# A padded memory layout: three of the activation's four sums moved from byte 320 to byte 0 modulo 512 of their partition

## The chip, the cores and the metric

The kernel runs on one core of one Trainium2 chip. The metric is device time in microseconds (us) for one execution, from numbers already in the chip's memory to the result written back. Lower is better. Inside the core, TensorE (PE) multiplies matrices, VectorE (DVE) and ScalarE (ACT) do elementwise work, GpSimd (POOL) does a little of it and issues some transfers, and SyncE (SP) issues most transfers. On-chip memory has 128 partitions; every tile has a start byte that is the same in each partition.

## The reference

The reference is two layers of an encoder on 512 tokens of width 1024, in float32. Each layer runs

```
h = h + 0.5 * post(SwiGLU(pre(h)))      first half-step feed-forward, d_ff = 2816
u = pre(h); three attention branches and three sigmoid gates from one projection of u
h = h + post((sum_i gate_i * (branch_i @ W_branch_i)) @ W_out)
h = h + 0.5 * post(SwiGLU(pre(h)))      second half-step feed-forward

swiglu(x) = (silu(x @ Wg) * (x @ Wu)) @ Wdown
```

where `pre` and `post` are RMS norms with a gain. Everything below is about the four feed-forward parts (two layers, two in each), and there about `x @ Wg` and `x @ Wu`.

## The kernel before

**Number format.** Every float32 operand `v` is divided into a high part `hi` (v rounded to the matmul's format by a copy on ACT) and a low part `lo = v - hi` (on DVE). One block product is three matmuls: hi·hi, hi·lo, lo·hi. A matmul has a stationary operand, 128x128, loaded by LDWEIGHTS, and a moving operand that streams 256 or 512 columns past it. Loading the next stationary operand overlaps the running matmul.

**Phases.** The program runs the phases f, m, f, f, m, f: `ffn` (kind "f") and `mixer` (kind "m", the attention). Each opens a pool of tiles for itself (`open_phase`, L130) which is laid over the pool of the phase before it; a new tile waits until the old tiles at its bytes are no longer used. Pools `sb` and `cp` live through the whole program. `cp` has constants, the identity for transposes among them.

**The feed-forward's products (`ffn`, L565 and on).** The activation x is held transposed, as features by tokens. The first blocks of a phase (6 in the first phase, 4 in the others; `plain`) are multiplied plainly, with 512 moving columns. The remaining `count = KF - plain` blocks (16 in the first phase, 18 in each of the others) are groups of a scheme with seven products instead of eight. The activation is cut into quadrants "11", "12", "21", "22" (feature half, token half), and four sums of them are made once per phase by `less` (L673 and on) and divided into hi and lo by `divide` (L668):

| sum | made of | hi and lo in tiles |
|---|---|---|
| t3 | 22 - 12 | ht3, lt3 |
| t1 | 11 - 12 | ht1, lt1 |
| t2 | -t3 - 11 | ht2, lt2 |
| t4 | -t2 - 21 | ht4, lt4 |

The work is put into the list `later`, from which one entry is taken at each step of four weight blocks while the plain blocks run (`step`, L210); what is left over is run after them. In the first phase the list also holds the normalized quadrants and copies for the residual (`normal`, `divide`, `keep`).

Each group g then has seven products, `p1` to `p7`, all through `product` (the matmuls are on line L848): 4 blocks of 128 features, 3 matmuls each, 12 matmuls of 256 columns. The stationary operand is a weight or a sum of weights, the moving one is a quadrant or a sum of quadrants:

| product | moving | stationary tiles |
|---|---|---|
| p1 | quadrant 11, tile X | h1, l1 |
| p7 | t3 | h13, l13 |
| p3 (of the group before) | quadrant 22, tile X | h24, l24 |
| p6 | t2 | h24, l24 |
| p4 | t4 | h1, l1 |
| p2 | quadrant 21, tile X | w12 (hi and lo) |
| p5 | t1 | h13, l13 |

This is also the order in which TensorE runs them, group after group; a group's last product is the one with t1. In the profile these rows are `mm<-X,h`, `mm<-X,l`, `mm<-ht,h`, `mm<-lt,h`, `mm<-ht,l` and, for p2 alone, `at<-X,w`. The first group of a phase has no p3 in its place; after the last group's p4 come p5, p2, p3. Between the matmuls DVE and ACT prepare the weights of the next group (`sum13`, `high1`, `low1` and the like, L699 to L737), copy and add products (L887 to L902) and write the gated result (L916). SP fetches two weight tiles of 512 KB a group.

After the groups, the second matrix is applied from L1088 (512 moving columns; the moving operands are weight tiles `wh`, `wl`, the stationary ones `f`, `f3x` and `part`), also with seven products and some plain ones; `part` with u = 2 is in "t" tiles (`settle`, L636 and on). The phase ends with the norm, transposes (L518) and the first matmuls of the next phase (`begin`), whose last weight tiles are kept in ht3 and lt3 (in the kernel's very first products in ht1 and lt1).

The order of instructions is the program's order with a planner that may move them; in the hand-over from one phase to the next the order is written out by hand (`ordered`).

**Where the tiles lie.** Tiles of a pool follow each other by the order of first use. All of the tiles here are multiples of 512 bytes long, so one pad at the front of the phase's pool sets the start of all of them modulo 512. The phase's pool begins at byte 116832 of the partition, which is 96 modulo 512; the pad of 184 words (736 bytes) makes it 832, or 320 modulo 512.

```
PAD = {"f": 184, "m": 184}
```

So before the change:

| tiles | pool | start modulo 512 |
|---|---|---|
| X (quadrants, `f`, `f3x`), weights wr, w12 and r13 (tags "wr", "wp") | sb | 0 |
| ht1 to ht4, lt1 to lt4 | phase | 320 |
| h1, l1, h13, l13, h24, l24, wh, wl (tag "x") | phase | 320 |
| a1, ap, t tiles | phase | 320 |

The rows of X and of the sums are 256 words, and the stationary blocks 128 words, so that each block within a tile keeps the tile's start modulo 512.

Of the kernel before, what the change touches and what calls it, by code (L numbers as in the profile page):

```python
# [10 lines left out]
F32 = mybir.dt.float32  # L11
# [5 lines left out]
P = 128  # L17
# [11 lines left out]
WB = 8  # L29
AHEAD = 2  # L30
WARM = 9
PAD = {"f": 184, "m": 184}
SECOND = 1
KS = 8
KP = KF - 2 * KS
# [80 lines left out]
def encoder_kernel(ctx: ExitStack, tc: tile.TileContext, order, xT, wts, cols, rows, rpb, consts, tables, out):  # L116
# [7 lines left out]
    phase = [None]  # L124
# [5 lines left out]
    def open_phase(kind):  # L130
        pool = ExitStack()
        phase[0] = (kind, pool.enter_context(tc.tile_pool(name=nm("ph"), bufs=1, reuse_waits="tile")))
        phase[0][1].tile([P, PAD[kind]], F32, tag="pad", name=nm("pad"), bufs=1)
        return pool
    serial = [0]

    def nm(s):
        serial[0] += 1
        return f"{s}{serial[0]}"

    def big(tag, dt=F32, shape=(P, T), name="v"):
        if tag in BUFS:
            return sb.tile(list(shape), dt, tag=tag, name=nm(name), bufs=BUFS[tag])
        kind, pool = phase[0]
        return pool.tile(list(shape), dt, tag=tag, name=nm(name), bufs=ABUFS[kind][tag])
# [4 lines left out]
    def bank(tag):  # L150
        return ps.tile([P, T], F32, tag=tag, name=nm(tag), bufs=PBUFS[tag])
# [3 lines left out]
    def f(t):  # L155
        return t.bitcast(F32)
# [30 lines left out]
    def fetch(parts, eng=None):  # L187
        raw = sb.tile([P, WB, P], F32, tag="wr", name=nm("wr"), bufs=BUFS["wr"])
        src = wts[len(stream["raw"])].rearrange("p (a b) -> p a b", b=P)
        for c in range(0, WB, WB // parts):  # L190
            cs = slice(c, c + WB // parts)
            (eng or stream["eng"]).dma_start(raw[:, cs, :], src[:, cs, :])
        stream["raw"].append(raw)
# [48 lines left out]
    for l in range(L):  # L242
        for which in (1, 2):
            name = f"ffn{which}_w_down"
# [37 lines left out]
    def first_loads(hT):  # L282
        def load(hs, *bs):
            for b in bs:
                nc.sync.dma_start(hT[:, b, hs], xT[b * P : (b + 1) * P, hs])

        load(HALVES[0], 0)
        fetch(2, nc.sync)
        load(HALVES[0], 1, 2)
        fetch(1, nc.sync)  # L290
        load(HALVES[0], 3, 4, 5)
        fetch(1, nc.sync)
        load(HALVES[0], 6, 7)
        load(HALVES[1], *range(KD))
        nc.sync.dma_start(cons, consts)
        warm = bank("o")
        for _ in range(WARM):
            PE.matmul(warm[:, :P], ones, ones, start=True, stop=True)
        V.tensor_scalar(out=half, in0=colt, scalar1=0.5, scalar2=None, op0=ALU.mult)
# [23 lines left out]
    def dense1(name, l, c, X, r0=0, tag="mm", midway=None):  # L323
        return dense([(name, l, r0, c)], X, (tag,), midway=midway)[0]
# [47 lines left out]
    def finish_rms(s, rB):  # L372
        V.tensor_copy(rB, inv_rms(s.acc, D, NT))
# [170 lines left out]
    def pair(name, dt=F32R):  # L544
        return big("x", dt, (P, 2, T), name=name)
# [19 lines left out]
    def ffn(l, which, X, accs):  # L565
# [3 lines left out]
        first = X is None  # L569
        plain = 6 if first else 4  # L570

        def z(tag, dt=F32R, shape=(P, 2, T)):
            return pool.tile(list(shape), dt, tag=tag, name=nm(tag), bufs=1)
# [8 lines left out]
        def two(ap):  # L582
            return ap.rearrange("p (a b) -> p a b", a=2)
# [3 lines left out]
        if first:  # L587
            hT = z("a1", F32, (P, KD, T))
            first_loads(hT)
            X = Operand(False)  # L590

            def operand(i):
                for b in range(KD):
                    src = hT[:, b, HALVES[i]]
                    p, q = (t[:, i, :] for t in X.blocks[b])
                    A.activation(p, src, AF.Copy, scale=gcol(b))
                    V.scalar_tensor_tensor(out=q, in0=src, scalar=gcol(b), in1=f(p), op0=ALU.mult, op1=ALU.subtract)

            operand(0)
            rowt = z("lt4", F32).rearrange("p a b -> p (a b)")[:, : L * ROWS].rearrange("p (a b) -> p a b", a=L)  # L600
            nc.sync.dma_start(rowt, rows.rearrange("(a b) -> a b", a=L)[:, :ROWS].partition_broadcast(P))
            between = lambda: operand(1)
        if first:
            stream["stop"] = len(order) // HB + 4 * plain
# [61 lines left out]
        later = stream["later"]  # L666
# [19 lines left out]
        def fetches(g):  # L686
            if g < count:
                W[g] = {}
                for _ in range(2):
                    fetch(1, nc.sync)  # L690
                raws[g] = [t.rearrange("p (a b) c -> p a b c", a=2) for t in stream["raw"][-2:]]

        def wpair(name):
            t = pair(name)
            return t.rearrange("p a (b c) -> p a b c", c=P)

        def sum13(g):
            W[g]["r13"] = sb.tile([P, 2, HB, P], F32, tag="wp", name=nm("r13"), bufs=BUFS["wp"])
            base = raws[g][1][:, 1].unsqueeze(1).to_broadcast([P, 2, HK, P])  # L699
            V.tensor_tensor(out=W[g]["r13"], in0=base, in1=raws[g][0], op=ALU.add)  # L700

        def high1(g):
            W[g]["h1"] = wpair("h1")
            A.activation(W[g]["h1"], raws[g][0], AF.Copy)
# [5 lines left out]
        def high13(g):  # L710
            W[g]["h13"] = wpair("h13")
            A.activation(W[g]["h13"], W[g]["r13"], AF.Copy)
# [26 lines left out]
        def some(*calls):  # L739
            return lambda: [c() for c in calls]  # L740

        def at(fn, *args):
            return lambda: fn(*args)

        def first_group():
            if stream["made"] < stream["stop"]:
                later.insert(0, first_group)
                return
            assert 2 * len(stream["raw"]) == stream["stop"]
            fetches(0)  # L750
            high1(0)
            sum13(0)
            high13(0)

        def quadrants(n):
            for i in range(2):
                for j in range(2):
                    raw[f"{i + 1}{j + 1}"] = n[i][:, j]

        if first:  # L760
            s = Squares()
            for hs in HALVES:
                for b in range(KD):
                    s.add(V, hT[:, b, hs], hs)
            rB = pair("rB", F32)[:, 0, :]
            u1 = dense1(gu, l, KF + 1, X.blocks, tag="at", midway=lambda: finish_rms(s, rB))
            prepare(rowt)
            n = [sb.tile([P, 2, HK, HT], F32, tag="n", name=nm("n"), bufs=BUFS["n"]) for _ in range(2)]
            own = [sb.tile([P, 2, HK, HT], F32R, tag="X", name=nm("X"), bufs=BUFS["X"]) for _ in range(2)]
            quadrants(n)  # L770

            def normal(b):
                V.scalar_tensor_tensor(
                    out=n[b // HK][:, :, b % HK, :], in0=two(hT[:, b, :]), scalar=gcol(b), in1=two(rB),
                    op0=ALU.mult, op1=ALU.mult,
                )

            def keep(tb):
                d = dr.tile([P, D], F32, tag="kept", name=nm("kept"), bufs=2 * NT)
                for i in range(2):  # L780
                    tp = bank("o")
                    for k in range(HB):
                        PE.transpose(tp[:, k * P : (k + 1) * P], hT[:, HB * i + k, tb * P : (tb + 1) * P], ident)
                    t = big("t", name="h")
                    A.activation(t, tp, AF.Copy)
                    nc.sync.dma_start(d[:, i * T : (i + 1) * T], t)
                kept.append(d)

            for b in range(0, KD, 2):
                later.append(some(at(normal, b), at(normal, b + 1)))  # L790
            later.append(at(divide, "11", own[0][:, 0], own[1][:, 0]))
            later.append(at(divide, "22", own[0][:, 1], own[1][:, 1]))
            later.extend(at(keep, tb) for tb in range(NT))
        else:
            quadrants(X.raw)
            for i, j in ((0, 0), (1, 0), (1, 1)):
                k = f"{i + 1}{j + 1}"
                hi[k], lo[k] = X.hi[i][:, j], X.lo[i][:, j]
# [2 lines left out]
                at(less, "t3", "22", "22", "12", 1),  # L801
                at(divide, "t3"),
                at(less, "t1", "12", "11", "12", 1),
                at(divide, "t1"),
                at(less, "t2", "t3", "t3", "11", -1),
                at(divide, "t2"),
                at(less, "t4", "t2", "t2", "21", -1),
# [877 lines left out]
    for l in range(L):  # L1685
        with open_phase("f"):
            X, accs = ffn(l, 1, X, accs)
        with open_phase("m"):
            X, accs = mixer(l, X, accs)
        with open_phase("f"):  # L1690
            X, accs = ffn(l, 2, X, accs)
# [59 lines left out]
```

## Time and profile before

| | |
|---|---|
| time, median of 3 executions | 2430.6 us (2428.65 to 2430.72) |
| time of the profiled execution | 2430.51 us |
| its span, first to last instruction | 2428.7 us |
| granted TensorE clock | 0.998 |
| PE busy | 2395.0 us (99%) |
| PE weight loads busy | 2098.5 us (86%) |
| DVE busy | 1787.3 us (74%) |
| ACT busy | 1343.8 us (55%) |
| POOL busy | 192.7 us (8%) |

A row of the groups' view names the line, the engine, the operation, output<-inputs with shapes, the count, the busy time in us, the mean of one in ns, and behind the bar the idle time before the group's instructions. A matmul's row counts from its issue to its modelled end, and matmuls are pipelined: the *pace* is therefore read from starts, in the timeline (start in us, duration in us, engine, line, operation, output<-inputs, count). A timeline row with "x2" stands for two matmuls of the same operands that follow each other, and its start is that of the first. In the chain of waits a row is a start, a duration and what ran.

### The profile page before, as it was taken

Reading aid. Unit: us, or ns where it says so; the run is one execution under the profiler, and the core shown is the slowest. Engines: PE = TensorE matmul, PEld = TensorE weight load, DVE = VectorE, ACT = ScalarE, POOL = GpSimd, SP = SyncE. Lnnn points to the kernel's source line nnn. Section 1 sums busy time; section 2 is a strip of 40 time slices with the busy share of each in tenths; the row PEclk is TensorE's granted clock in tenths of the full one; section 3 lists DMA queues with packets and bytes.
Section 4 is the critical chain, followed back from the end, with each engine's and each line's share of the span. In section 5 each row is a group of like instructions: output and inputs, shape, how many; then the busy total and the mean of one; then the engine's idle time right before and its main releaser. Section 6 shows DMA issues by size and latency. Waiting matters only on the chain. (4 is left out here: it accounts for less than half of the span.)

```text
span 2428.7 us, 37745 instructions
## 1 busy us (share of the span) xinstructions
PE 2395.0 (99%) x14266; PEld 2098.5 (86%) x14266; DVE 1787.3 (74%) x2959; ACT 1343.8 (55%) x2487; POOL 192.7 (8%) x192
## 2 busy tenths in 40 slices
PE   9999999999999999999999999999999999999998
PEld 8999887888777889998899998878887778899987
DVE  8887975857667467888878878767676764788786
ACT  6554655646555365555655554555565554556553
POOL 0111000001111101110001110000011111011100
PEclk9999999999999999999999999999999999999999
DMA  5566536435443324664425565364454333346642
GB/s 171 162 164 183 166 131 178 126 105 152 117 122 97 120 96 146 159 157 165 168 92 157 157 174 191 114 176 117 115 146 127 112 97 120 99 146 164 181 146 90
DMA packets 119190, 340.46 MB, mean 140 GB/s; under 512 B 15968, under 2 KB 22752, under 8 KB 118496
## 3 DMA queue, kind: packets, MB, share of 16 engines
q1 hardware_dynamic: 91344, 224.72, 30.0%
q10 hardware_dynamic: 22032, 79.78, 11.1%
q0 software_dynamic: 5632, 33.56, 6.8%
q8 instruction: 112, 1.84, 0.3%
q14 instruction: 70, 0.57, 0.1%
HBM read 285.03 MB, written 48.23 MB: 137 GB/s over the span
## 5 line engine op out<-in xcount | busy, mean ns | idle before, releaser
L304 PE MATMUL mm<-X,w 128*128 128x512 f32 (+1 forms) x1044 | 396.5, 380 | 1.9 <-ACT w L205 1.3
L305 PE MATMUL mm<-X,w 128*128 128x512 f32 (+1 forms) x1044 | 397.1, 380 | 0.8 <-DVE X L528 0.7
L306 PE MATMUL mm<-X,w 128*128 128x512 f32 (+1 forms) x1044 | 396.7, 380 | 0.0
L206 DVE TENSOR_TENSOR w<-wr,w 128x512 fp32r<-128x512 f32 x360 | 255.7, 716 | 168.9 <-ACT w L205 167.3
L205 ACT ACTIVATE w<-wr 128x512 fp32r<-128x512 f32 x360 | 223.5, 627 | 224.0 <-PE mm L306 180.4
L848 PE MATMUL mm<-ht,l 128*128 128x256 f32 x1120 | 316.0, 282 | 0.0
L848 PE MATMUL mm<-ht,h 128*128 128x256 f32 x1120 | 315.9, 282 | 0.0
L848 PE MATMUL mm<-lt,h 128*128 128x256 f32 x1120 | 315.0, 281 | 0.0
L304 PEld LDWEIGHTS mm<-X,w 128*128 128x128 f32 x1044 | 197.3, 189 | 34.5 <-ACT w L205 1.7
L305 PEld LDWEIGHTS mm<-X,w 128*128 128x128 f32 x1044 | 197.2, 189 | 32.9 <-DVE X L528 1.1
L306 PEld LDWEIGHTS mm<-X,w 128*128 128x128 f32 x1044 | 197.1, 189 | 31.0
L848 PEld LDWEIGHTS mm<-ht,l 128*128 128x128 f32 x1120 | 212.8, 190 | 0.0
L848 PEld LDWEIGHTS mm<-ht,h 128*128 128x128 f32 x1120 | 212.7, 190 | 0.1
L848 PEld LDWEIGHTS mm<-lt,h 128*128 128x128 f32 x1120 | 212.5, 190 | 0.0
L1088 PE MATMUL mm<-wh,f 128*128 128x512 f32 x640 | 200.4, 391 | 0.0
L848 PE MATMUL mm<-X,h 128*128 128x256 f32 x1120 | 200.4, 278 | 0.0
L848 PEld LDWEIGHTS mm<-X,h 128*128 128x128 f32 x1120 | 171.1, 189 | 0.4
L848 PE MATMUL mm<-X,l 128*128 128x256 f32 x560 | 155.1, 277 | 0.0
L1088 PEld LDWEIGHTS mm<-wh,f 128*128 128x128 f32 x640 | 120.2, 188 | 27.1
L708 DVE TENSOR_TENSOR l<-wr,h 128x1024 fp32r<-128x1024 f32 x70 | 85.7, 1224 | 77.4 <-PE mm L848 77.4
L1088 PE MATMUL mm<-wl,f 128*128 128x512 f32 x320 | 126.4, 395 | 3.1 <-DVE wl L965 3.1
L330 ACT ACTIVATE hi<-at 128x256 fp32r<-128x256 f32 (+2 forms) x168 | 73.9, 453 | 73.3 <-PE at L1381 34.2
(370 smaller groups left out, 5427.8 us busy)
## 6 DMA issues: line engine op xcount, KB each, us to landing
wr<-in_wts_dram SPq DMA_DIRECT2D x223, 512.0 KB, 4.6
wr<-in_wts_dram ACTq DMA_DIRECT2D x152, 512.0 KB, 3.6
sum<-in_wts_dram POOLq DMA_DIRECT2D x64, 512.0 KB, 5.4
st<-hi SPq DMA_DIRECT2D x84, 128.0 KB, 2.3
st<-lo SPq DMA_DIRECT2D x84, 128.0 KB, 3.0
ap<-in_wts_dram SPq DMA_DIRECT2D x20, 512.0 KB, 7.1
a<-kept SPq DMA_DIRECT2D x32, 256.0 KB, 5.9
ap<-sum SPq DMA_DIRECT2D x16, 512.0 KB, 3.3
```

The lines of the kernel that those rows point to most:

```text
L205: A.activation(hi, raw, AF.Copy)
L206: V.tensor_tensor(out=lo, in0=raw, in1=f(hi), op=ALU.subtract)
L304: PE.matmul(acc, w[0], x[0], start=start, stop=False)
L305: PE.matmul(acc, w[0], x[1], start=False, stop=False)
L306: PE.matmul(acc, w[1], x[0], start=False, stop=stop)
L330: A.activation(hi, src, AF.Copy)
L708: V.tensor_tensor(out=W[g]["l1"], in0=raws[g][0], in1=f(W[g]["h1"]), op=ALU.subtract)
L848: PE.matmul(acc, ws[i], xs[j], start=start and k == n == 0, stop=stop and k == HK - 1 and n == 2, skip_group_check=True,)
L1088: PE.matmul(acc, x[i], w[j], start=start and n == 0, stop=stop and n == 2, skip_group_check=True)
```

## The change

The pad at the front of an "f" pool becomes 104 words, so that the pool's tiles begin at 0 modulo 512. Tiles of 80 words (320 bytes) and 48 words (192 bytes), which nothing reads or writes, are put between the others. `gap` makes them. In the phases other than the first, ht3, lt3, the t tiles and ap then begin at 0; "gap1" takes ht1 and lt1 to 320, "gap2" takes ht2, lt2, ht4, lt4 back to 0, and "gapx" takes the "x" tiles and a1 to 320. In the first phase, where the order of first use is another, a1 and lt4 begin at 0, "gap1" takes ht1, lt1, the t tiles, the "x" tiles and ap to 320, and "gaph" takes ht3, lt3, ht2, lt2 and ht4 to 0. The m pools and `sb` stay as they are. No instruction is added or removed. In the first phase "gaph" is one more entry of `later`, so that the entries behind it are taken one step later.

```diff
-PAD = {"f": 184, "m": 184}
+PAD = {"f": 104, "m": 184}
...
+    def gap(tag, w):
+        phase[0][1].tile([P, w], F32, tag=tag, name=nm(tag), bufs=1)
...
             nc.sync.dma_start(rowt, rows.rearrange("(a b) -> a b", a=L)[:, :ROWS].partition_broadcast(P))
+            gap("gap1", 80)
             between = lambda: operand(1)
...
             fetches(0)
+            if not first:
+                gap("gapx", 80)
             high1(0)
             sum13(0)
...
             later.extend(at(keep, tb) for tb in range(NT))
+            later.append(at(gap, "gaph", 48))
         else:
...
                 at(less, "t3", "22", "22", "12", 1),
                 at(divide, "t3"),
                 at(less, "t1", "12", "11", "12", 1),
-                at(divide, "t1"),
+                some(at(gap, "gap1", 80), at(divide, "t1"), at(gap, "gap2", 48)) if not first else at(divide, "t1"),
                 at(less, "t2", "t3", "t3", "11", -1),
                 at(divide, "t2"),
                 at(less, "t4", "t2", "t2", "21", -1),
```

## The prediction

> **What bounds the kernel now.** I read the page first, then the groups, then the chain of waits over the last phase's groups. From the page:
>
> ```profile
> span 2428.7 us, 37745 instructions
> PE 2395.0 (99%) x14266; PEld 2098.5 (86%) x14266; DVE 1787.3 (74%) x2959; ACT 1343.8 (55%) x2487; POOL 192.7 (8%) x192
> L848 PE MATMUL mm<-ht,l 128*128 128x256 f32 x1120 | 316.0, 282 | 0.0
> L848 PE MATMUL mm<-ht,h 128*128 128x256 f32 x1120 | 315.9, 282 | 0.0
> L848 PE MATMUL mm<-lt,h 128*128 128x256 f32 x1120 | 315.0, 281 | 0.0
> L848 PE MATMUL mm<-X,h 128*128 128x256 f32 x1120 | 200.4, 278 | 0.0
> L708 DVE TENSOR_TENSOR l<-wr,h 128x1024 fp32r<-128x1024 f32 x70 | 85.7, 1224 | 77.4 <-PE mm L848 77.4
> ```
>
> TensorE is busy from end to end, and the products' matmuls (L848) had no idle time before them. DVE's low part of the next weights (L708) is what waits, for TensorE. The chain shows what that means: it lies on TensorE through every group, one group after another in a fixed period.
>
> ```profile
> 2135.72 8.47 PE mm L848 x72
> 2144.19 1.42 PE at L848 x12
> 2145.61 8.47 PE mm L848 x72
> 2154.08 1.42 PE at L848 x12
> ```
>
> A group is 84 matmuls and lasts 2145.61 - 2135.72 = 9.89 us. So the groups are bound by the pace at which TensorE takes matmuls, and every nanosecond of that pace goes into the time.
>
> The page's four L848 rows differ although the shapes are equal. The pace itself is in the timeline; these are starts in the first phase, one group with the first row of the next:
>
> ```profile
> 168.15 0.40 PE L848 MATMUL mm<-X,h 128*128 128x256 f32 x2
> ...
> 168.73 0.28 PE L848 MATMUL mm<-X,l 128*128 128x256 f32 x1
> ...
> 169.53 0.28 PE L848 MATMUL mm<-ht,h 128*128 128x256 f32 x1
> ...
> 170.94 0.40 PE L848 MATMUL mm<-X,h 128*128 128x256 f32 x2
> ...
> 171.53 0.28 PE L848 MATMUL mm<-X,l 128*128 128x256 f32 x1
> ...
> 172.32 0.28 PE L848 MATMUL mm<-ht,h 128*128 128x256 f32 x1
> ...
> 173.75 0.28 PE L848 MATMUL mm<-ht,h 128*128 128x256 f32 x1
> ...
> 175.19 1.58 PE L848 MATMUL at<-X,w 128*128 128x256 f32 x12
> ...
> 176.60 0.28 PE L848 MATMUL mm<-ht,h 128*128 128x256 f32 x1
> ...
> 178.03 0.40 PE L848 MATMUL mm<-X,h 128*128 128x256 f32 x2
> ```
>
> The differences of the first rows are the products: p1 1.38, p7 1.41, p3 1.38, p6 1.43, p4 1.44, p2 1.41, p5 1.43 us, in all 9.88. I set beside them where the operands lie modulo 512, moving first: p1 and p3 (0, 320); p7, p6, p4, p5 (320, 320); p2 (0, 0). The products whose two operands start at *different* places are the quick ones. Within them the pace settles: from the sixth matmul on, p1 takes (169.53 - 168.73)/7 = 114 ns and p3 (172.32 - 171.53)/7 = 113 ns a matmul. p4, which comes after p6 with the same places, takes 1.44/12 = 120 ns throughout. So the groups have a quick pace, 113.3 ns, and a slow one, 120 ns, and p7, p6, p2 and p5 are mixtures, on the way from one to the other.
>
> Different places are not enough, though. There are products with (0, 320) that are not quick: the first p1 of a phase, and the last group's p3 (the row after it is the next stage):
>
> ```profile
> 80.08 0.40 PE L848 MATMUL mm<-X,h 128*128 128x256 f32 x2
> ...
> 81.50 0.28 PE L848 MATMUL mm<-ht,h 128*128 128x256 f32 x1
> ...
> 237.36 0.40 PE L848 MATMUL mm<-X,h 128*128 128x256 f32 x2
> ...
> 238.66 0.28 PE L848 MATMUL mm<-X,l 128*128 128x256 f32 x1
> ```
>
> They take (81.50 - 80.08)/12 = 118 and (238.66 - 237.36)/11 = 118 ns. Both come right after matmuls with (0, 0). The quick ones, p1 and p3 in the groups, come after (320, 320). So the pace also depends on what ran before.
>
> **The change part by part.**
>
> *p7, p3, p6, p4.* After the change p7, p6 and p4 have (0, 320), like p1 and p3. p5, with t1 left at 320, keeps (320, 320), and the next group's p1 comes after it as before: it should settle at the quick pace as now. Then p7, p3, p6 and p4 find nothing changed between one product and the next, and I let them keep the quick pace: 12 x 113.3 ns = 1.36 us each.
>
> *p2 and p5.* p2 then comes after a quick product, not a slow one. No row shows (0, 0) after the quick pace. Its bounds are 1.36 (it stays quick) and 1.44 us (slow throughout); p7, which leaves the quick pace for a slow pair of places, takes 1.41, and I take 1.42. p5 comes after p2 as before: 1.43.
>
> *A group:* 1.38 + 4 x 1.36 + 1.42 + 1.43 = 9.67 us, against 9.885 now: 0.215 us less. The 16 + 3 x 18 = 70 groups make 15 + 3 x 17 = 66 full turns after each phase's first: 66 x 0.215 = 14.2 us. In a first turn p1 stays at 118, after (0, 0); p7, p6 and p4 should then keep 118 (1.41 instead of 1.44, some 0.08 us a phase, 0.3 us in all). Gain 14.5 us; with p2's bounds, 13.2 to 18.5.
>
> *Does TensorE stay the bound?* A window over one full group of the last phase (busy us of PE, PEld, DVE, ACT, POOL), and what p3 and p6 there have to wait for, DVE's addition to the group before and ACT's copy of p1:
>
> ```profile
> 2155.49:2165.38 9.89, 9.89 (x87) 9.89 (x86) 7.98 (x11) 5.51 (x9) 1.47 (x2) 1.00 0.54 155
> ```
> ```profile
> 2147.48 0.42 DVE L902 TENSOR_TENSOR v<-mm,v 128x256 f32<-128x256 f32 x1
> ...
> 2148.87 0.37 ACT L887 ACTIVATE at<-mm 128x256 f32<-128x256 f32 x1
> ...
> 2149.68 0.40 PE L848 MATMUL mm<-X,h 128*128 128x256 f32 x2
> ...
> 2151.05 0.28 PE L848 MATMUL mm<-ht,h 128*128 128x256 f32 x1
> ```
>
> DVE has 7.98 us of work for 9.67; p3 starts 2149.68 - 2147.90 = 1.78 us after its addition, p6 2151.05 - 2149.24 = 1.81 us after its copy, and both come only some 0.07 us sooner. The cover is ample, so the gain passes on whole.
>
> *What becomes slower.* The last weights before a new phase's products (tiles ht3, lt3) move from 320 to 0, and their moving operand X is at 0; the second matrix's `part` tiles with u = 2 move likewise in three phases, beside moving operands at 320. Rows for both:
>
> ```profile
> 1571.31 0.28 PE L304 MATMUL at<-X,ht 128*128 128x256 f32 x1
> ...
> 1574.14 0.40 PE L304 MATMUL mm<-X,w 128*128 128x512 f32 x1
> ```
> ```profile
> 300.35 0.39 PE L1088 MATMUL at<-wh,part 128*128 128x512 f32 x1
> ...
> 310.88 0.39 PE L1088 MATMUL at<-wl,part 128*128 128x512 f32 x1
> ...
> 311.57 0.39 PE L1088 MATMUL at<-wl,part 128*128 128x512 f32 x1
> ...
> 316.55 0.39 PE L1088 MATMUL at<-wh,part 128*128 128x512 f32 x1
> ```
>
> The first: 24 matmuls in 2.83 us, 118 ns, which would be 120 as (0, 0): 2 x 24 in three hand-overs x 2 ns = 0.3 us. The second: (320, 0) takes 10.53/46 = 229 ns, (320, 320) 4.98/22 = 226 ns; 2 x 24 x 3 = 144 matmuls x 2.5 ns = 0.35 us. Transposes whose stationary tile moves (some 160) have no row with it at 0; by the 7 ns between the two paces that is 1.1 us either way, and I take nothing.
>
> *Waits.* With starts shifted by 320 bytes a tile now touches three old tiles instead of two. The one place that I find where a queue could feel it is the hand-over to the second attention phase, on SP:
>
> ```profile
> 1573.34 0.42 SPq L1410 DMA_DIRECT2D sinR<-in_tables_dram  x1
> 1574.37 0.80 SPq L1413 DMA_DIRECT2D mask<-in_tables_dram  x2
> 1575.29 0.47 SPq L1311 DMA_DIRECT2D st<-hi  x1
> ```
>
> sinR now touches lt3 too, whose last reader ends where the mask's wait ends, at 1574.37. So sinR, the masks and the copies `st<-hi` behind them on SP come 0.42 us later. TensorE has the next dense products to run meanwhile; bounds 0 to 0.4 us, taken as 0. The extra entry of `later` puts the first phase's last sums one step later, 12 matmuls of 512 columns, at 229 ns some 2.7 us. Its last division ended long before the groups began at 80.08:
>
> ```profile
> 64.12 1.21 DVE L671 TENSOR_TENSOR lt<-n,ht 128x1024 fp32r<-128x1024 f32 x1
> ```
>
> 15 us of cover. For DVE and ACT no row sets 0 against 320 in one operation; L708 already reads at 0 and writes at 320, and a loss there of a few ns in 1224 would lie in the 1.8 us of cover. I take nothing.
>
> *Sum.* 14.5 - 0.3 - 0.35 = 13.85 us. The profiled execution took 2430.51 us (span 2428.7 and 1.8 around it), 0.1 under the median: 2430.5 - 13.85 = **2416.7 us**.
>
> **The rivals.**
>
> *Only some of the sums gain.* The chain from p1 to p4 must keep the quick pace over sixty matmuls, and the tiles differ above bit 9. If p7 stayed at 1.41 (so that p3 falls back to 1.38), p6 and p4 still go to 1.36: 0.14 us a group, 9 us, 2422. If only p4 gained, 0.08 us, 5 us, 2426. For it: every quick row so far has an X tile. Against: X tiles at several places are all quick.
>
> *No change.* Either the quick pace is lost, so that the whole chain runs at the 118 of a phase's first p1: 5 x 1.41 + 1.42 + 1.43 = 9.90 for 9.885, 2431; or the place of an operand does not matter and the X products are quick for another reason, 2430.5. The second is what the Trainium skill would make of it ("TensorE: Matmul & The Clock Gate", section "Step-by-step: what each phase is for"): TensorE reads its moving operand and its weights through two independent ports, and loading the next weights takes no read bandwidth from the running matmul. By that rule nothing in this change could move the pace. The trace does not agree so far: p1 and p4 have the same shape and the same stationary tiles h1 and l1, and take 1.38 and 1.44.
>
> *Slower.* The quick pace may be the after-effect of alternating places: in the kernel before it is never kept for more than one product. If four more products at the same places wear it off, and it decays to the slow 120 ns, then p7, p3, p6, p4 cost 1.44 each: 9.99 for 9.885, 66 x 0.105 = 6.9 us more, with the 0.65 above 2438. It decides once the decay comes within p7. Against it: from the sixth to the twelfth matmul of p1 and p3 there is no drift, and (0, 320) at 118 shows no decay to 120 over 24 matmuls (1571.31 to 1574.14).
>
> **How the numbers follow.** The forecast has 0.77, "only some" 0.09, "no change" 0.09, "slower" 0.05. Its own range is p2's bounds and the transposes: 2412 to 2420. To leave out no more than 2 in 10 the range takes in the first of the partial cases: 2411.5 to 2423.5. A measurement here can tell about 0.2% (4.9 us) from no change. Faster by more: the forecast, and most of "only some", 0.84. Within 0.2%: 0.11. Slower by more: 0.05.
>
> **What would show it.** Right: the chain's period goes from 9.89 to about 9.67 us in all four phases; p7, p3, p6, p4 start 1.36 us apart; p1 stays at 1.38 and p5 at 1.43; L848 still has no idle time before it. Wrong: a period of 9.8 to 9.9 with products at 1.41 (the quick pace not kept), or above 9.9; or idle time on TensorE before p3 or p6, with DVE or ACT named; or a later first attention matmul at a hand-over. If the period falls as said and the time does not, the gain went at the phases' borders.

## The result

The kernel with the change took 2415.74 us (median of 4 runs, 2413.36 to 2417.91) against 2430.14 us for the kernel before on the same chip: a ratio of 0.9941, with a 95% interval of 0.993 to 0.9953. That is 14.4 us less; the prediction was 2416.7, 13.85 less. The same kernel, timed again on its own (the first of the runs below), took 2416.67 us.

The profiled execution of after took 2413.36 us, with a span of 2411.6. Line numbers are up to 8 higher than before: the products' L848 is now L856, L1088 is L1096, L902 is L910, L708 is L713, L304 is L308. From the page of after:

```profile
span 2411.6 us, 37743 instructions
PE 2379.9 (99%) x14266; PEld 2084.2 (86%) x14266; DVE 1782.5 (74%) x2959; ACT 1342.9 (56%) x2487; POOL 193.2 (8%) x192
L856 PE MATMUL mm<-ht,l 128*128 128x256 f32 x1120 | 311.1, 278 | 0.0
L856 PE MATMUL mm<-ht,h 128*128 128x256 f32 x1120 | 311.1, 278 | 0.0
L856 PE MATMUL mm<-lt,h 128*128 128x256 f32 x1120 | 310.9, 278 | 0.0
L856 PE MATMUL mm<-X,h 128*128 128x256 f32 x1120 | 199.1, 277 | 0.0
L713 DVE TENSOR_TENSOR l<-wr,h 128x1024 fp32r<-128x1024 f32 x70 | 85.7, 1224 | 70.9 <-PE mm L856 70.9
```

Each engine has as many instructions as before (the total in the first row is two lower). TensorE still has no idle time before its products, and the rows with ht and lt went from 281 or 282 to 278 ns: the three sums' products now look like those of the X tiles (277). DVE's low parts of the weights still wait for TensorE, 70.9 instead of 77.4 us. The chain of waits over the last phase's groups (start, length, what):

```profile
2141.57 8.25 PE mm L856 x72
2149.82 1.44 PE at L856 x12
2151.25 8.25 PE mm L856 x72
2159.51 1.44 PE at L856 x12
```

The period is 2151.25 - 2141.57 = 9.68 us for 9.89 before. The six products that were 8.47 us together take 8.25; p2, alone in its row, went up from 1.42 to 1.44. The timeline of a group in the first phase, the rows that start p1, p7, p2, p5 and the next p1:

```profile
167.21 0.40 PE L856 MATMUL mm<-X,h 128*128 128x256 f32 x2
...
168.59 0.28 PE L856 MATMUL mm<-ht,h 128*128 128x256 f32 x1
...
174.03 1.60 PE L856 MATMUL at<-X,w 128*128 128x256 f32 x12
...
175.47 0.28 PE L856 MATMUL mm<-ht,h 128*128 128x256 f32 x1
...
176.90 0.40 PE L856 MATMUL mm<-X,h 128*128 128x256 f32 x2
```

p1 takes 1.38 us, p7, p3, p6 and p4 together 174.03 - 168.59 = 5.44, 1.36 each, p2 1.44, p5 1.43. Taken to the nanosecond from the starts, as medians over the full groups:

| ns | p1 | p7 | p3 | p6 | p4 | p2 | p5 | group |
|---|---|---|---|---|---|---|---|---|
| before | 1379 | 1421 | 1379 | 1421 | 1441 | 1415 | 1431 | 9887 |
| after | 1379 | 1360 | 1360 | 1360 | 1360 | 1437 | 1431 | 9687 |

How much of the time this is, TensorE's busy time on the products' line alone says, summed over the four phases, first of before, then of after:

```profile
sum 2450.00, PE 693.62; mean PE 173.41
```
```profile
sum 2450.00, PE 679.98; mean PE 170.00
```

The loops lost 13.64 us (13.92 in the second profile of the same kernel, whose sum is 679.70). The medians of the two comparisons fell by 14.4 and 13.4 us. So the gain is in the loops; what the profiled execution shows beyond it (its span fell by 17.1 us) is mostly between the loops, where the attention lies and executions differ by as much. From the end of the third feed-forward part's products to the start of the fourth's, with the second attention between, it took 687.4 us in the profile of before, 685.1 and 684.9 in the two of the change, and 683.4 to 688.2 in the kernels of the runs below.

### The profile page after: what moved, and what is told of

The parts are those of the page before. It is cut to its first block, busy times and chain, and to the rows that moved or that the text cites. A ratio compares the mean times of both kernels' runs of the same rounds, so it can differ in the third digit from the quotient of the medians.

```text
span 2411.6 us, 37743 instructions
## 1 busy us (share of the span) xinstructions
PE 2379.9 (99%) x14266; PEld 2084.2 (86%) x14266; DVE 1782.5 (74%) x2959; ACT 1342.9 (56%) x2487; POOL 193.2 (8%) x192
## 5 line engine op out<-in xcount | busy, mean ns | idle before, releaser
L308 PE MATMUL mm<-X,w 128*128 128x512 f32 (+1 forms) x1044 | 396.0, 379 | 2.6 <-ACT w L209 1.2
L856 PE MATMUL mm<-ht,l 128*128 128x256 f32 x1120 | 311.1, 278 | 0.0
L856 PE MATMUL mm<-ht,h 128*128 128x256 f32 x1120 | 311.1, 278 | 0.0
L856 PE MATMUL mm<-lt,h 128*128 128x256 f32 x1120 | 310.9, 278 | 0.0
L308 PEld LDWEIGHTS mm<-X,w 128*128 128x128 f32 x1044 | 196.8, 189 | 35.0 <-ACT X L531 1.4
L856 PEld LDWEIGHTS mm<-ht,h 128*128 128x128 f32 x1120 | 210.8, 188 | 0.0
L856 PEld LDWEIGHTS mm<-ht,l 128*128 128x128 f32 x1120 | 210.8, 188 | 0.0
L856 PEld LDWEIGHTS mm<-lt,h 128*128 128x128 f32 x1120 | 210.8, 188 | 0.0
L1096 PE MATMUL mm<-wh,f 128*128 128x512 f32 x640 | 201.3, 393 | 0.0
L856 PE MATMUL mm<-X,h 128*128 128x256 f32 x1120 | 199.1, 277 | 0.0
L856 PEld LDWEIGHTS mm<-X,h 128*128 128x128 f32 x1120 | 170.1, 188 | 0.5 <-DVE v L910 0.2
L856 PE MATMUL mm<-X,l 128*128 128x256 f32 x560 | 154.9, 277 | 0.0
L1096 PEld LDWEIGHTS mm<-wh,f 128*128 128x128 f32 x640 | 120.3, 188 | 26.3
L713 DVE TENSOR_TENSOR l<-wr,h 128x1024 fp32r<-128x1024 f32 x70 | 85.7, 1224 | 70.9 <-PE mm L856 70.9
L1096 PE MATMUL mm<-wl,f 128*128 128x512 f32 x320 | 125.4, 392 | 3.1 <-DVE wl L973 3.1
```

The lines of the kernel that those rows point to most:

```text
L308: PE.matmul(acc, w[0], x[0], start=start, stop=False)
L713: V.tensor_tensor(out=W[g]["l1"], in0=raws[g][0], in1=f(W[g]["h1"]), op=ALU.subtract)
L856: PE.matmul(acc, ws[i], xs[j], start=start and k == n == 0, stop=stop and k == HK - 1 and n == 2, skip_group_check=True,)
L1096: PE.matmul(acc, x[i], w[j], start=start and n == 0, stop=stop and n == 2, skip_group_check=True)
```

## The experiments

In the tables "loops" is that sum of TensorE's busy time on the products' line, and "outside" the measured time less the loops: 2430.1 - 693.6 = 1736.5 us for the kernel before, 2415.7 - 680.0 = 1735.8 for after. (a, b) are the places of the moving and the stationary operand modulo 512, as in the prediction. Each ratio is against the kernel before on the same chip, whose median there was 2429.9 to 2431.2 us. Diffs are against the kernel with the change.

**1. The change once more.** No edit.

> The changed kernel once more, for its time beside the others of this set and to see which differences between two of its executions are not the change. Theory (the pace of a product depends on whether its two operands start at the same place modulo 512, and on what ran before): every full group lasts 9.69 us again (p1 1.38, p7, p3, p6, p4 1.36, p2 1.44, p5 1.43), and the groups of the four phases last 13.6 us less than before; the whole is 2414 to 2418, and what varies between executions lies in the attention phases. Rival (the first profile's 17 us were all the change's): the span is 2412 again.

2416.67 us (2414.69 to 2417.6), ratio 0.9941 (0.9926 to 0.9956); every product as in the table above to 1 ns. The paces are properties of the layout, not of one execution. The span was 2412.9 us, near the rival's 2412, but the medians of the two comparisons fell by only 14.4 and 13.4 us: the first profile's 17 us weren't all the change's.

**2. All four sums at 0.** The one sum that the change leaves at 320, t1 for p5, goes to 0 too.

```diff
-            gap("gap1", 80)
             between = lambda: operand(1)
@@ behind the first products of the first phase
+            gap("gap1", 80)
@@
-                some(at(gap, "gap1", 80), at(divide, "t1"), at(gap, "gap2", 48)) if not first else at(divide, "t1"),
+                at(divide, "t1"),
```

> The fourth sum (t1, of a group's last product p5) begins at byte 0 as well; weights stay at 320. Theory: p5 then has different places, but comes right after p2 with (0, 0), and nothing in a group has equal places at 320 any more. Matmuls with (0, 320) after (0, 0) took 118 ns so far and kept it. So p5, p1, p7, p3, p6 and p4 should all run at 118: 6 x 1.41 + 1.44 = 9.92 us a group instead of 9.69, and the time goes to 2431 to 2434, all of the gain lost. Rival (different places are quick whatever ran before): p5 1.36, p1 1.36 and a group of 9.60 us, 2410.

2432.85 us, ratio 1.0008 (0.9998 to 1.0017); the chain over its last phase:

```profile
2154.09 8.48 PE mm L856 x72
2162.57 1.44 PE at L856 x12
```

A period of 9.92 us. Six of the seven products have (0, 320), as the quick ones of the change, and all of them take 1.41 us: 118 ns a matmul, group after group, for 18 groups. So the pace isn't set by the places of the operands alone. p2, with (0, 0), puts TensorE into the 118 ns pace for whatever has (0, 320) behind it, and in the change it is p5, with (320, 320), that takes it out again. The first phase's first group shows p2's part by itself: a short halt ahead of p6 was followed by one quick product, p4 with 1360 ns, and after the p2 behind it all went on at 118. The sum left at 320 costs its own product 1.43 instead of 1.36 us and keeps the five others at 1.36 to 1.38: the whole gain of the change hangs on it.

**3. Everything at 0.** The pads of the change without its gaps: the sums, the groups' weights and the rest of the phase's tiles all at 0.

```diff
-            gap("gap1", 80)
@@
-            if not first:
-                gap("gapx", 80)
@@
-            later.append(at(gap, "gaph", 48))
@@
-                some(at(gap, "gap1", 80), at(divide, "t1"), at(gap, "gap2", 48)) if not first else at(divide, "t1"),
+                at(divide, "t1"),
```

> The phase's pool begins at byte 0 with no tiles between, so that sums and weights in it are both at 0 like X. Theory: equal places everywhere, every product at 120 ns: 7 x 1.44 = 10.08 us a group against 9.89 before, 13 us more in the groups; the second matrix's matmuls become (0, 0) instead of (320, 0), 227 instead of 229 ns, some 3 us less: 2439 to 2444. Rival (an operand that starts at byte 0 is the quick one): all products at 1.36, a group of 9.52 us, 2405.

2439.43 us, ratio 1.0036 (1.0022 to 1.0051), slower than before:

```profile
2153.68 8.64 PE mm L852 x72
2162.32 1.44 PE at L852 x12
```

10.08 us, 120 ns a matmul in every product. Byte 0 isn't quick as such; two operands at one place are slow here at 0, as before the change at 320.

**4. Four other places for the three sums.** Only the numbers in the pad and in the gaps change, so that t1, the weights and everything else stay where the change has them (at 256, for instance):

```diff
-PAD = {"f": 104, "m": 184}
+PAD = {"f": 40, "m": 184}
@@
-            gap("gap1", 80)
+            gap("gap1", 16)
@@
-                gap("gapx", 80)
+                gap("gapx", 16)
@@
-            later.append(at(gap, "gaph", 48))
+            later.append(at(gap, "gaph", 112))
@@
-                some(at(gap, "gap1", 80), at(divide, "t1"), at(gap, "gap2", 48)) if not first else at(divide, "t1"),
+                some(at(gap, "gap1", 16), at(divide, "t1"), at(gap, "gap2", 112)) if not first else at(divide, "t1"),
```

At 288, 32 bytes from the weights:

> Three sums at 288 instead of 0, 32 bytes away from the weights at 320; t1 at 320. Theory A (any two different places modulo 512 will do): as with 0, p7, p3, p6, p4 at 1.36 us and a group of 9.69. Theory B (the places have to differ by about half of 512, or in a coarser unit such as 64): p7, p6, p4 stay at 1.41 to 1.44, a group of 9.8 to 9.9 us. Note that X stays at 0, so that p7 and p6 now alternate with other places than p1 and p3.

At 256:

> The sums t2, t3, t4 begin at 256 modulo 512, 64 bytes from their weights at 320; t1 and the rest as in the change. Theory D (the quick pace needs a distance of a few tens of bytes, more than the 32 that sums288 showed to be too little): if 64 is enough, p7, p3, p6, p4 take 1.36 us, a group 9.69, the time about 2416; if it is not, 1.41 to 1.42 each as at 288, a group 9.90, about 2429. Theory Z (it is the place 0 of the moving operand that counts, not the distance): 9.90, about 2429.

At 192:

> The sums t2, t3, t4 begin at 192 modulo 512, 128 bytes from their weights at 320. Theory D with a threshold of 128 or less: p7, p3, p6, p4 at 1.36 us, a group 9.69, about 2416; with a threshold between 128 and 192 (0 and 320 are 192 apart modulo 512): 9.90, about 2429. Theory Z: 9.90, about 2429.

At 64:

> The sums t2, t3, t4 begin at 64 modulo 512, 256 bytes from their weights at 320, the farthest that there is modulo 512. Theory D, whatever its threshold: p7, p3, p6, p4 at 1.36 us, a group 9.69, about 2416. Theory Z: 1.41 to 1.42 each, a group 9.90, about 2429. This run tells the two apart.

| the sums at | p7 | p3 | p6 | p4 | p2 | group, ns | loops, us | time, us (one run) |
|---|---|---|---|---|---|---|---|---|
| 288 | 1414 | 1414 | 1419 | 1419 | 1424 | 9900 | 694.3 | 2428.8 |
| 256 | 1360 | 1360 | 1360 | 1360 | 1437 | 9687 | 679.8 | 2416.7 |
| 192 | 1428 | 1385 | 1428 | 1423 | 1432 | 9906 | 694.7 | 2430.8 |
| 64 | 1421 | 1379 | 1421 | 1441 | 1415 | 9887 | 693.5 | 2429.3 |

The first run, the oldest of the four, says that not just any different place will do. Of the theories of the other three neither holds. 256 is the change again, product for product. 64, the farthest from 320 that there is, is the kernel *before* again, product for product, where the sums lay at 320 themselves; its chain:

```profile
2154.09 8.47 PE mm L856 x72
2162.56 1.42 PE at L856 x12
```

So neither the distance nor byte 0 counts. 0 and 256 are alike, and 64 and 320 are alike: 0 and 4 units of 64 bytes, 1 and 5 units. This suggested the theory of the next runs: a matmul is quick where its two operands begin in units of 64 bytes of *different parity*, one even and one odd (theory P). 288 begins in the middle of a unit and is between. 192 is an odd unit and slow, as it should be, though its 1428 is not the 1421 of 64: parity isn't all that counts.

**5. The X tiles at 64.** Two spare tiles, 64 bytes ahead of the X tiles and 448 behind them.

```diff
+            sb.tile([P, 16], F32, tag="gapX", name=nm("gapX"), bufs=1)
             X = Operand(False)
+            sb.tile([P, 112], F32, tag="gapW", name=nm("gapW"), bufs=1)
```

> The layout of the change, and the X tiles begin at 64 modulo 512 (two spare tiles, ahead of the first X and behind it, move nothing else). p1 and p3 become (64, 320), p2 becomes (64, 0), and the dense products with X move too; p7, p6, p4 stay at (0, 320). If a distance of 64 bytes is enough (theory D), p2 no longer slows down: about 1.36 instead of 1.44, p5 then about 1.42, a group 9.60 instead of 9.69, 66 x 0.086 = 5.7 us less, about 2410. If more than 64 is needed, p2 stays at 1.42 to 1.44 and the group at 9.69, about 2416. Theory Z: p1 and p3 lose the quick pace, p1 1.43 and p3 1.41 to 1.42, while p7 enters the quick pace at 1.38: a group about 9.80, about 2424.

2421.23 us, ratio 0.9961 (0.9947 to 0.9975). The products took, in their order, 1440, 1379, 1421, 1379, 1360, 1362 and 1439 ns, a group 9780. Its timeline in the second phase, the starts of p2 and p5:

```profile
1016.39 1.52 PE L858 MATMUL at<-X,w 128*128 128x256 f32 x12
...
1017.75 0.28 PE L858 MATMUL mm<-ht,h 128*128 128x256 f32 x1
```

p2, (64, 0), takes 1.36 us instead of 1.44, and p1, (64, 320), 1.44 instead of 1.38. Parity says both: odd with even is quick, odd with odd is slow. Theory Z's group of 9.80 comes near the 9.78 measured, but it has no reason for a quick p2. The loops sum to 685.1, outside 1736.1.

**6. One sum alone.** Only t4 at 0; t1, t2 and t3 at 320 as before the change (`phase[1]` counts the phases opened).

```diff
-        phase[0][1].tile([P, PAD[kind]], F32, tag="pad", name=nm("pad"), bufs=1)
+        phase[0][1].tile([P, 104 if phase[1] == 1 else 184], F32, tag="pad", name=nm("pad"), bufs=1)
@@
-            later.append(at(gap, "gaph", 48))
@@
-                some(at(gap, "gap1", 80), at(divide, "t1"), at(gap, "gap2", 48)) if not first else at(divide, "t1"),
+                at(divide, "t1"),
@@
-                at(divide, "t4"),
+                some(at(gap, "gap4", 48), at(divide, "t4")),
```

> One part of the change alone: only the sum t4 (moved by p4) begins at 0 modulo 512, t1, t2 and t3 stay at 320 as before. Theory P (a matmul is quick where the starts of its two operands lie in 64-byte units of different parity, and each product enters its pace from the one before): p7 1.42, p3 1.38, p6 1.42 as before, p4 enters the quick pace as p1 does, 1.38 instead of 1.44, p2 after it 1.44 instead of 1.415; a group 9.85 for 9.89, 66 x 0.04 = 2.6 us, about 2427.5. If the chain as a whole were needed for the quick pace, p4 would stay at 1.41 to 1.44 and the time at 2430.

The products came out as expected: p4 1379, p2 1437, the others as before, a group of 9847; the loops 690.6, 3.0 us less than before. The single time, 2430.63 us, doesn't show these 3 us (13 runs of the kernel before beside it went from 2428.07 to 2434.12); in this execution the stretch with the second attention was the longest of all, 688.2 us. One sum gains by itself, then: p4 saves 62 ns, and p2 gives 22 of them back. In the whole change p4 saves 81, and p3 19 that it doesn't save here, because they no longer have to enter the quick pace.

**7. The weights of p2 at an odd unit.** By theory P the slow p2 is worth 77 ns a group. Its weights lie in a ring of four buffers at 0 that the plain matmuls use too. Each buffer gets 128 bytes more, and p2's weights begin 64 bytes into theirs.

```diff
-        t = sb.tile([P, 2, HB, P], dt, tag="wp", name=nm(name), bufs=BUFS["wp"])
-        return t[:, 0], t[:, 1]
+        t = wtile(name, dt, at).rearrange("p (a b c) -> p a b c", a=2, b=HB)
+        return t[:, 0], t[:, 1]
+    def wtile(name, dt, at=0):
+        t = sb.tile([P, 2 * T + 32], dt, tag="wp", name=nm(name), bufs=BUFS["wp"])
+        return t[:, at : at + 2 * T]
@@
-            W[g]["h12"], W[g]["l12"] = wpart("w12")
+            W[g]["h12"], W[g]["l12"] = wpart("w12", at=16)
```

> The layout of the change, and the weights of p2 (h12, l12) lie 64 bytes into their buffers, at an odd multiple of 64 (64, 192, 320 or 448 modulo 512) instead of 0; the other tiles of that ring begin at 0, 128, 256 or 384. Theory P: p2 keeps the quick pace, 1.36 instead of 1.44; p5 then goes slow from the start, 1.44 as in x64; p1 1.38: a group 1.38 + 5 x 1.36 + 1.44 = 9.62 for 9.69, 66 x 0.068 = 4.5 us less than the change, about 2411.5. If the pace hung on the exact places seen so far and not on the parity: p2 at 1.42 to 1.44, a group 9.69, about 2416.

p2 takes 1360, p5 1421, a group 9600 ns: the loops sum to 673.0, 7.0 us less than with the change. The time is 2416.28 us, ratio 0.9941 (0.9926 to 0.9956), no less than with the change. Outside the loops it went up from 1736 to 1743.3. The place is in the plain matmuls of 512 columns, whose weights are in the same ring: here are the first and the last of one stretch of 120 of them, in the second run of the change and in this kernel (119 steps):

```profile
893.29 0.40 PE L308 MATMUL at<-X,w 128*128 128x512 f32 x1
...
920.29 0.39 PE L310 MATMUL at<-X,w 128*128 128x512 f32 x1
```
```profile
895.31 0.40 PE L312 MATMUL at<-X,w 128*128 128x512 f32 x1
...
922.84 0.40 PE L314 MATMUL at<-X,w 128*128 128x512 f32 x1
```

27.00 / 119 = 226.9 ns against 27.53 / 119 = 231.3. By buffer, over all of them: 232.9 ns where the weights begin at 128 or 384, 230.2 at 0 or 256, and 228.8 in the kernel with the change, where all begin at 0. There are some 3,000 such matmuls, so on average 2.8 ns more each make some 8 us, which covers the 7. All four places are even units: for 512 columns parity isn't enough. What p2 gained, the matmuls that share its ring lost.

**8. Every pair apart.** X at 64, all four sums at 320, the groups' weights at 384, those of p2 and of the plain matmuls at 128.

```diff
-PAD = {"f": 104, "m": 184}
+PAD = {"f": 152, "m": 152}
@@
+            sb.tile([P, 16], F32, tag="gapX", name=nm("gapX"), bufs=1)
             X = Operand(False)
+            sb.tile([P, 16], F32, tag="gapW", name=nm("gapW"), bufs=1)
@@
-            gap("gap1", 80)
@@
-                gap("gapx", 80)
+                gap("gapx", 16)
@@ ahead of the first tile of the groups' weights in the first phase
+            gap("gapx", 16)
@@
-            later.append(at(gap, "gaph", 48))
+            later.append(at(gap, "gaph", 112))
@@
-                some(at(gap, "gap1", 80), at(divide, "t1"), at(gap, "gap2", 48)) if not first else at(divide, "t1"),
+                at(divide, "t1"),
```

> Every product's moving operand at an odd multiple of 64 (X at 64, all four sums at 320), every weight tile of the groups at an even one (384, and 128 for those of p2). Theory P, and a quick pace that can be entered after a hand-over: 84 x 113.3 ns = 9.52 us a group, 0.167 less than with the change, 66 x 0.167 = 11.0 us, about 2405. Rival: as in four_at_0, where after the dense matmuls nothing slow ever broke the 118 ns pace, the groups stay at 118 throughout: 9.90 to 9.92, about 2431.

2431.21 us, ratio 1.0006 (0.9996 to 1.0015). Both theories were right, in different phases. From the starts of p1 to the next p1, in the first phase and in the second:

```profile
165.76 0.39 PE L858 MATMUL mm<-X,h 128*128 128x256 f32 x2
...
175.28 0.39 PE L858 MATMUL mm<-X,h 128*128 128x256 f32 x2
...
1011.07 0.40 PE L858 MATMUL mm<-X,h 128*128 128x256 f32 x2
...
1020.96 0.28 PE L858 MATMUL mm<-X,h 128*128 128x256 f32 x1
```

9.52 us, 84 matmuls at 113.3 ns, the quickest group of all runs; and 9.89 us, 84 at 118 ns. The groups' code and their places modulo 512 are the same. The first phase's groups came in at the quick pace and kept it for all 16 groups, the other three came in at 118 and kept that. The state is older than the first product. Two matmuls of 512 columns, with both operands in X, run right ahead of a phase's first p1. In the twelve phases of runs 7 to 9 they took 464 to 467 ns together in the six where that p1 was quick (1360 to 1372 ns), and 452 to 458 in the six where it took 1413 or 1414. What sets their pace no run shows. Outside the loops the time is 1744.0: the ring at 128 has its cost here too (the same stretch takes 233.4 ns a matmul).

**9. A layout drawn from all this.** X at 64, three sums at odd units, the weights of the groups at 384, the ring of the plain matmuls left at 0, and t1 alone at 384, beside its weights, to break the 118 ns pace.

```diff
-PAD = {"f": 104, "m": 184}
+PAD = {"f": 184, "m": 184}
@@
+            sb.tile([P, 16], F32, tag="gapX", name=nm("gapX"), bufs=1)
             X = Operand(False)
+            sb.tile([P, 112], F32, tag="gapW", name=nm("gapW"), bufs=1)
@@
-            gap("gap1", 80)
+            gap("gap1", 16)
@@
-                gap("gapx", 80)
+                gap("gapx", 112)
@@
-            later.append(at(gap, "gaph", 48))
+            later.append(at(gap, "gaph", 16))
@@
-                some(at(gap, "gap1", 80), at(divide, "t1"), at(gap, "gap2", 48)) if not first else at(divide, "t1"),
+                some(at(gap, "gap1", 16), at(divide, "t1"), at(gap, "gap2", 16)) if not first else at(divide, "t1"),
```

> A layout drawn from the runs: X at 64, the sums t2, t3, t4 at 320 or 448 (odd multiples of 64), the weights of the groups at 384 and those of p2 at 0 (even), and only t1 beside its weights, at 384. So p5 alone is slow, as with the change, and the weight ring of the dense matmuls stays at 0, since in p2_64 and all_apart, where it had moved to 128 modulo 256, the matmuls of 512 columns took some 233 instead of 229 ns. Theory P: p1 1.38, five products at 1.36, p5 1.42: a group 9.60, as in p2_64 and 0.087 under the change; the loops 672 to 674 us for 679, and with what x64 took outside the loops (2421.2 - 684.5 = 1736.7) about 2410. Rival: if the slow product p5 (384, 384) does not break the 118 ns pace that all_apart kept in three of its four phases, the groups there stay at 9.90 and the time at about 2424.

2423.58 us (2422.56 to 2426.48), ratio 0.9971 (0.9959 to 0.9982): quicker than before, slower than the change. That is the rival's number, but not by the rival's way. t1 did break the pace: p1 after it takes 1379 in all four phases. The starts of p7, p6 and p2 in the second phase:

```profile
1012.04 0.28 PE L858 MATMUL mm<-ht,h 128*128 128x256 f32 x1
...
1014.76 0.28 PE L858 MATMUL mm<-ht,h 128*128 128x256 f32 x1
...
1017.59 1.57 PE L858 MATMUL at<-X,w 128*128 128x256 f32 x12
```

p7, whose sum t3 lies at 320 there, and p3 take 2.72 us together, 1.36 each. p6 and p4, whose sums lie at 448, take 2.83, 118 ns a matmul (in the first phase, where t3 lies at 448, p7 too takes 1413 ns), and p2, (64, 0), which was quick in run 5 behind a quick product, stays at 118 behind them. (448, 384) is odd with even, and not quick. Theory P falls as a rule for all places: of the odd units, 448 (or 192, its place modulo 256) isn't like 64 and 320. I had taken 448 to save room, as one odd unit for another. With these two sums at 320 all pairs but p5's would be ones that a run has shown to be quick; that layout wasn't run.

The paces seen at 256 columns, over all runs, in ns a matmul:

| moving, stationary | pace |
|---|---|
| (0, 320), (256, 320), (64, 384), (320, 384), (64, 0), (64, 128), and 0 with weights at an odd unit for p2 in run 7, as a rule behind a quick product or behind (320, 320), (64, 320) or (384, 384) | 113.3 |
| (0, 320) behind (0, 0); (448, 384) behind a quick one; (64, 0) behind (448, 384); (288, 320) | 118 |
| (64, 384), (320, 384), (64, 128), in three of the four phases of run 8 | 118 |
| (192, 320) | 119 |
| (0, 0), (320, 320), (384, 384), (64, 320) | 120, once settled |

## Why the prediction was right, point by point

**What bounds the kernel.** Right: what the change moves is TensorE's pace in the groups. Runs 1 to 4 change only places in memory, and the time follows the loops: outside them it is 1733 to 1738 us in every one of these kernels, while the time goes from 2415.7 to 2439.4.

**p7, p3, p6, p4.** Right: 1360 ns each, as predicted, by the quick pace handed on from p1. That t1 has to stay at 320 for this was part of the step ("it should settle at the quick pace as now"), and run 2 shows it: without it the change would have gained nothing.

**p2.** Here a size was off. The prediction took 1.42 us because p7, when it left the quick pace, took 1.41; it measured 1.437, the upper end of its bounds of 1.36 and 1.44. Behind a quick product (0, 0) is slow from the first matmul on (119, then 120), and p7 in the kernel before, (320, 320) behind the quick p1, took eight matmuls to get there (120, 112, 117, 118, 119, 121, 117, 117, then 120). The wrong part was that the way into the slow pace is the same for every slow pair. It cost 17 ns x 66 = 1.1 us.

**p5.** Right: 1.43 predicted, 1431 measured. The group is 9.687 us for 9.67 predicted, the fall 0.200 for 0.215.

**The first turns.** Right in the three later phases. In the second phase p1, p7, p6 and p4 ran from

```profile
919.74 0.40 PE L856 MATMUL mm<-X,h 128*128 128x256 f32 x2
...
925.39 1.60 PE L856 MATMUL at<-X,w 128*128 128x256 f32 x12
```

5.65 us / 48 = 118 ns, as the prediction had it behind (0, 0). In the first phase TensorE halted some 60 ns at p6 and went on at 113: behind a short halt the 118 ns pace can be over. Behind another, of some 0.3 us, in the second turn p3, p6 and p4 went back to 118. Neither is worth 0.3 us.

**The costs.** The last weights at a hand-over, and SP's queue there:

```profile
1560.22 0.28 PE L308 MATMUL at<-X,ht 128*128 128x256 f32 x1
...
1563.10 0.40 PE L308 MATMUL mm<-X,w 128*128 128x512 f32 x1
```
```profile
1563.33 0.33 SPq L1418 DMA_DIRECT2D sinR<-in_tables_dram  x1
1563.71 0.90 SPq L1421 DMA_DIRECT2D mask<-in_tables_dram  x2
```

24 matmuls in 2.88 us, 120 ns, for 118 before: the price that was predicted. sinR now does wait for lt3, and the masks are issued 0.61 us after the matmul that follows lt3's last one (1563.71 - 1563.10), instead of 0.23 (1574.37 - 1574.14): 0.38 us later, for 0.42 predicted. TensorE has dense matmuls to run there and goes on without a gap for 25 us more. Its first wait in the attention then is 0.94 us long before, 1.25 and 0.84 in the two profiles of the change: nothing of the 0.38 us can be seen, and taking it as 0 was right. The `part` tiles with u = 2 take 229 ns a matmul from start to start (24 of them in the third phase), as the prediction had it. All matmuls of the second matrix together cost 0.27 us more, for 0.35 predicted.

**The cover.** Right. The addition before p3 in the last phase, and p3:

```profile
2143.43 0.42 DVE L910 TENSOR_TENSOR v<-mm,v 128x256 f32<-128x256 f32 x1
...
2145.57 0.39 PE L856 MATMUL mm<-X,h 128*128 128x256 f32 x2
```

p3 starts 2145.57 - 2143.85 = 1.72 us after its addition has ended, 0.06 less than before, for 0.07 predicted; p6 has as much behind its copy.

**The sum.** The gain in the loops came out at 13.64 us for the 14.5 predicted; p2's 1.1 us is more than the difference. Against it stood costs of 0.65, taken rightly at their size, but what happens outside the loops varies by more than that from execution to execution, and the two medians fell by 14.4 and 13.4. That the forecast came within 1 us of the first is partly luck of that kind; its terms hold to about 1 us each.

**The rivals.** "Only some of the sums gain" didn't come about, but run 6 shows that a gain in part is possible: one sum, moved alone, gains 40 ns a group. "No change" in its first form, everything at the 118 of a phase's first p1, is what run 2 does, 2432.85 for the 2431 that the prediction gave it: it was the place of one sum away. Its second form, the rule of the Trainium skill ("TensorE: Matmul & The Clock Gate", section "Step-by-step: what each phase is for") that the moving operand and the weights are read through two independent ports, would have had all of these kernels at one time. The runs don't agree with that: nothing but where the tiles begin differs between run 1 and run 3, and they take 2416.67 and 2439.43 us at a granted clock of 0.999. "Slower", the wearing off of the quick pace, is out: run 8 kept it for 16 groups.

## What to carry to other kernels

Where matmuls stream one after another and the profile gives different mean times to rows of one shape, set the start bytes of the moving and the stationary tile beside each of them: here that alone moved the time by 1% over the layouts tried, with no instruction changed. Judge a layout by the whole sequence, since the pace of a product hangs on the one before it and a slow product can be what keeps five others quick. And move a tile in a shared ring only after costing everything else that reads from that ring.

## What was not expected of the hardware

- The start bytes count in a pattern much finer than 512: 64 gives the paces of 320 and 256 those of 0, to 1 ns. At 256 columns different parity in units of 64 bytes goes with the quick pace in all pairs tried but (448, 384) and, for 288, a place inside a unit. What in the chip makes it so, and why 448 is an exception, stays open; so does which layout is best.
- The same pairs of places have two stable paces, 113.3 and 118 ns, and the matmuls stay in the one they entered for as long as only such pairs follow and no halt comes between: 18 groups, 178 us, in run 8. So the pace has a memory that is longer than any one product.
- Matmuls of 512 columns have their own pattern: 226.9 ns for (0, 0), 228.9 for (64, 0) (run 5) and 233.4 for (64, 128) (run 8), in the same stretch. With 256 columns (64, 0) is the quick one and (0, 0) the slow one.
